# 24 of the 32 FFN down products in pairs by Strassen's seven products, with operands kept in DRAM, and merge planes loaded through staging

## The chip, the core and the metric

One core of one Trainium2 chip runs the whole program. TensorE multiplies, VectorE (DVE) and ScalarE (ACT) work element by element, GpSimd (POOL) and SyncE (SP) here mostly start transfers, and 16 DMA engines move data between DRAM and the on-chip memory. Each engine takes its instructions in a fixed order and waits where an input is not there yet. The metric is device time in microseconds of one execution, the median of several.

## What is computed

One step of a one-layer hybrid decoder for 1024 prompt tokens and 8 sample tokens, in 32-bit floating point. The part that the change concerns comes at the end of the layer:

```python
u  = sigmoid(ga + bma) * (o_hg @ w_br_a) + sigmoid(gb + bmb) * (y @ w_br_b)   # merge
x  = x + g1 * (u @ w_out)
h2 = rmsnorm(x, norm_mlp) * (1 + sc2) + sh2
x  = x + g2 * (square(relu(h2 @ w_up)) @ w_down)       # 1024 -> 4096 -> 1024
y  = rmsnorm(x, norm_final)
```

## The kernel before

**Layout.** Activations are kept transposed: a plane is 128 features (partitions) by 1032 token columns (1024 of the prompt, 8 samples). 1024 features are 8 planes (KD = 8). A 32-bit value is split in two float32r parts, hi (a rounded copy by ACT) and lo (the rest, a subtraction by DVE); a product of two such operands is three matmuls: wh by lo, wl by hi, wh by hi.

**A dense product** (`dense`, `dense_split`, L78 to L97) makes one output plane of 128 features from 8 input planes. `load_w` (L46) brings a 128x1024 weight block through one of three staging buffers `wr` (`stage`, L42) and splits it into `wh` (ACT, L53) and `wl` (DVE, L55); each of these has two buffers. The columns are done in three slices of 344, so a product is 3 x 8 x 3 = 72 matmuls of 344 columns, all on L86. PSUM has three `acc` banks for it. `DenseK` (L99) does the same work input plane by input plane (matmuls on L114), so that it can begin while later planes are still being loaded; it occupies all three `acc` banks until it ends.

**A Strassen pair** (`strassen_pair`, L1076) makes two output planes at once by seven products of half-size blocks (Winograd's form with few sums) in the order 1, 7, 6, 2, 5, 4, 3. Each product is two column quarters (q = 0, 1) of 258, of 4 x 3 = 12 matmuls each: 168 matmuls of 258 columns for a pair, on L1103. `strassen_weights` (L1035) forms the sums of the weight blocks and their splits (DVE on L1049 and L1061, ACT on L1059 to L1071) in tiles that share the two `wh` and two `wl` buffers. Products 1, 6 and 7 are copied out of PSUM by ACT (`keep`, L1092) before their bank goes on accumulating; products 2, 5, 4 and 3 each complete a quarter of the output, which `evac` takes out.

**The order of the work** is laid down at build time by a planner that gives each engine its sequence: of the instructions whose inputs it takes to be ready, the one that stands first in the program, where code inside `high_priority(AHEAD)` counts as standing 2000 instructions earlier. Weight loads and splits, evacuations and the sums of `strassen_weights` all stand in such blocks, so among them the place in the program decides. Matmuls, the sums of squares and the final norm have their plain place. The engines then keep the planned order, whatever really comes late.

**The stages in order.** `phase_merge` (L872): the two branch products and the gates. Each input plane is loaded by `load_split` (L837), which sends the raw data straight to the place of the lo plane and splits it there (ACT L844, DVE L845). `phase_out` (L961): the `w_out` product, x1 (8 planes that stay on the chip) and h2. `phase_ffn` (L1118): 32 up products, the first six dense (during which the sums of h2 for Strassen are made), then 13 Strassen pairs; the squared relu of each quarter is made in `evac` (DVE L1158, L1159, L1133; ACT L1132) and stored in DRAM, `ad`, by SP (L1129). Then 32 down products, 8 for each of four chunks c of 1024 inner features, all dense; planes of `ad` are loaded back and split (`act`, L1166, by `load_split`), 8 for the first chunk just when the down stage begins. Each product is added to x1 under its gate (`gated_add`, L933, DVE L937). The last chunk goes by column slices: for each of three slices 8 products, whose squares are summed (`sum_sq`, L950, L951), then the final norm (`rstd_model`, L1195) and the store of the output.

**Planes on the chip.** `PlanePool` (L1203) has planes under the names A (16), D (4), E (6) and L (14); a new plane takes the place of an older one when all its readers are done.

Of the kernel before, what the change touches and what calls it, by code (L numbers as in the profile page):

```python
# [17 lines left out]
P = 128  # L18
T = 1024
NB = 8  # L20
# [25 lines left out]
def load_w(k, src, prio=AHEAD):  # L46

    nc = k.nc
    with k.tc.high_priority(prio):
        wr = stage(k)[:, :KD * P]  # L50
        nc.sync.dma_start(wr, src)
        wh = k.wp.tile([P, KD * P], F32R, tag="wh", name="wh", bufs=2)
        nc.scalar.activation(wh, wr, AF.Copy)  # L53
        wl = k.wp.tile([P, KD * P], F32R, tag="wl", name="wl", bufs=2)
        nc.vector.tensor_tensor(wl, wr, wh.bitcast(F32), op=ALU.subtract)  # L55
    return wh, wl
# [42 lines left out]
class DenseK:  # L99


    def __init__(self, k, srcs, evacs, n=KD, prio=AHEAD):
        self.k, self.evacs, self.n, self.i = k, evacs, n, 0
        self.ws = [load_w(k, src, prio) for src in srcs]
        self.accs = [[k.ps.tile([P, 512], F32, tag="acc", name="acc", bufs=3) for _ in range(NS)],
                     [rec_ps(k, "acc2") for _ in range(NS if len(srcs) > 1 else 0)]]
# [730 lines left out]
def load_split(k, src, tag):  # L837
# [95 lines left out]
def gated_add(k, s, dst, base, ps, gate):  # L933

    nc = k.nc
    n = SW if s < NS - 1 else SW - NB
    nc.vector.scalar_tensor_tensor(dst[:, :n], ps[:, :n], gate[:, 0:1], base[:, :n], ALU.mult, ALU.add)  # L937
    if n < SW:
        t = k.sp.tile([P, NB], F32, tag="ga", name="ga", bufs=2)
        nc.vector.tensor_tensor(t, ps[:, n:], gate[:, 1:9], op=ALU.mult)  # L940
        nc.vector.tensor_tensor(dst[:, n:], t, base[:, n:], op=ALU.add)

# [133 lines left out]
def strassen_pair(k, srcs, X, evac):  # L1076
# [18 lines left out]
    for p, b in ((1, 1), (7, 2), (6, 1), (2, 3), (5, 1), (4, 2), (3, 1)):  # L1095
        for q in range(2):
# [8 lines left out]
            with k.tc.high_priority(AHEAD):  # L1105
# [8 lines left out]
                else:  # L1114
                    evac(0, 1, q, None, acc)


def phase_ffn(k, x1, h2):  # L1118
    nc = k.nc
    NF = 4 * KD  # L1120
    up = k.i["w_up"]
    ad = [k.dp.tile([P, NT], F32, name="ad%d" % j) for j in range(NF)]
    bufs = iter(range(1 << 20))

    def out(j, cols):
        n = next(bufs) % 4
        pool, tag = (k.sp2, "mt") if n < 2 else (k.sp, "sq")
        r = pool.tile([P, SW], F32, tag=tag, name="r", bufs=2)[:, :cols.stop - cols.start]
        return r, lambda: nc.sync.dma_start(ad[j][:, cols], r)  # L1129

    def relu2(r, ps):
        nc.scalar.activation(r, ps, AF.Relu)  # L1132
        nc.vector.tensor_tensor(r, r, r, op=ALU.mult)  # L1133

    def evac_up(j):
        def f(s, ps):
            r, store = out(j, cs(s))
            relu2(r, ps)
            store()
# [11 lines left out]
    for n in range(6, NF, 2):  # L1151
        def evac(m, half, q, a, ps, n=n):
            c = half * HN + q * HQ
            r, store = out(n + m, slice(c, c + HQ))
            if a is None:
                relu2(r, ps)
            else:
                nc.vector.tensor_tensor(r, a, ps, op=ALU.add)  # L1158
                nc.vector.scalar_tensor_tensor(r, r, 0.0, r, ALU.max, ALU.mult)  # L1159
            store()  # L1160
        strassen_pair(k, (up[n], up[n + 1]), X, evac)
# [4 lines left out]
    def act(c, j):  # L1166
        tag = "A" if c % 2 == 0 else "Q2" if j < 4 else "Q3"
        return load_split(k, ad[c * KD + j], tag)
    down = k.i["w_down"]
    aX = []  # L1170
    d = DenseK(k, (down[0],), (add(0),))
    for j in range(KD):
        with k.tc.high_priority(AHEAD):
            aX.append(act(0, j))
        d.step(*aX[j])
    for c in range(4):
        nX = []
        for m in range(KD):
            if c == 3:
                break  # L1180
            if c or m:
                dense(k, down[c * KD + m], aX, add(m))
            nX.append(act(c + 1, m))
        if c < 3:
            aX = nX
    for s in LAST:
        acc = k.sp2.tile([P, SW], F32, tag="sqa", name="sqa", bufs=1)
        for m in range(KD):
            w = load_w(k, down[3 * KD + m])
# [182 lines left out]
```

## Time and profile before

| | us |
|---|---|
| median of 3 runs (2532.47 to 2538.55) | 2536.15 |
| the profiled execution | 2534.51 |
| its span, first to last instruction | 2532.7 |
| TensorE busy | 2477.3 (98%) |
| DVE busy | 1754.1 (69%) |
| ACT busy | 1064.2 (42%) |

The profile is of one execution. A busy time counts instructions from start to end; consecutive matmuls overlap, so how fast TensorE goes is read from how many matmuls begin in a stretch, not from their durations. In the same way DVE instructions that do not depend on each other begin some 0.08 us before the one ahead has ended. The stages stand in these places of the span: merge from 1437, w_out from 1723, up products from 1816, the 13 Strassen pairs from 1884.8 to 2146.4, down products from 2146.4 to 2519.5, and the end of the last norm and stores to 2532.7.

### The profile page before, as it was taken

Reading aid. Unit: us, or ns where it says so; the run is one execution under the profiler, and the core shown is the slowest. Engines: PE = TensorE matmul, PEld = TensorE weight load, DVE = VectorE, ACT = ScalarE, POOL = GpSimd, SP = SyncE. Lnnn points to the kernel's source line nnn. Section 1 sums busy time; section 2 is a strip of 40 time slices with the busy share of each in tenths; the row PEclk is TensorE's granted clock in tenths of the full one; section 3 lists DMA queues with packets and bytes.
Section 4 is the critical chain, followed back from the end, with each engine's and each line's share of the span. In section 5 each row is a group of like instructions: output and inputs, shape, how many; then the busy total and the mean of one; then the engine's idle time right before and its main releaser. Section 6 shows DMA issues by size and latency. Waiting matters only on the chain.

```text
span 2532.7 us, 47468 instructions
## 1 busy us (share of the span) xinstructions
PE 2477.3 (98%) x19782; PEld 2409.1 (95%) x19782; DVE 1754.1 (69%) x3513; ACT 1064.2 (42%) x1574; POOL 4.2 (0%) x16
## 2 busy tenths in 40 slices
PE   6999999999999999999999999999999999999998
PEld 5999999989999999999999899999999999999997
DVE  7788888886678687787787733356976666443356
ACT  4455555554453544544535522123533334221123
POOL 0000000000000000000000000000000000000000
PEclk9999999999999999999999999999999999999999
DMA  6322222223334243243344634223233335332234
GB/s 256 125 95 98 94 99 102 101 97 101 102 110 139 82 145 128 97 148 120 101 145 135 229 111 151 76 101 125 98 109 112 105 105 158 129 116 84 75 103 147
DMA packets 114678, 300.94 MB, mean 119 GB/s; under 512 B 19056, under 2 KB 41648, under 8 KB 114448
## 3 DMA queue, kind: packets, MB, share of 16 engines
q1 hardware_dynamic: 113920, 296.91, 34.9%
q8 instruction: 155, 2.54, 0.4%
q0 software_dynamic: 112, 0.66, 0.1%
q14 instruction: 59, 0.48, 0.1%
q10 hardware_dynamic: 432, 0.35, 0.0%
HBM read 241.02 MB, written 57.10 MB: 118 GB/s over the span
## 4 chain that ended last, share of the span: by engine, by line
PE 73%; DVE 2%; DMA 1%; ACT 1%; issue 0%; SPq 0%; DVEq 0%; ACTq 0%
PE acc L86 56%; PE b L1103 10%; PE y_ps L795 1%; PE acc L114 1%; PE yi_ps L799 1%; PE kvx_ps L759 1%; DMA lo<-od 1%; PE xt_ps L747 1%; PE cb_ps L729 1%; DVE wl L55 1%; DMA lo<-ad 1%; DMA gt<-gd 0%; PE btok_ps L722 0%; PE ss L160 0%; ACT wh L53 0%
## 5 line engine op out<-in xcount | busy, mean ns | idle before, releaser
L86 PE MATMUL acc<-hl,wh 128*128 128x344 f32 x2232 | 721.8, 324 | 0.0
L86 PE MATMUL acc<-hh,wl 128*128 128x344 f32 x2232 | 721.1, 323 | 0.2 <-DVE wl L55 0.2
L86 PE MATMUL acc<-hh,wh 128*128 128x344 f32 x2232 | 717.2, 321 | 0.0
L86 PEld LDWEIGHTS acc<-hh,wh 128*128 128x128 f32 x2232 | 420.2, 188 | 2.9 <-issue 1.6
L86 PEld LDWEIGHTS acc<-hh,wl 128*128 128x128 f32 x2232 | 419.3, 188 | 3.8 <-issue 1.4
L86 PEld LDWEIGHTS acc<-hl,wh 128*128 128x128 f32 x2232 | 419.3, 188 | 3.4
L86 PE MATMUL acc<-hi,wl 128*128 128x344 f32 x1224 | 392.8, 321 | 2.3 <-DVE wl L55 2.3
L86 PE MATMUL acc<-lo,wh 128*128 128x344 f32 x1224 | 391.5, 320 | 1.4 <-ACT wh L53 1.4
L86 PE MATMUL acc<-hi,wh 128*128 128x344 f32 x1224 | 391.5, 320 | 0.0
L53 ACT ACTIVATE wh<-wr 128x1024 fp32r<-128x1024 f32 x198 | 208.8, 1055 | 416.0 <-PE acc L86 358.5
L55 DVE TENSOR_TENSOR wl<-wr,wh 128x1024 fp32r<-128x1024 f32 x198 | 242.1, 1223 | 202.7 <-ACT wh L53 201.6
L86 PEld LDWEIGHTS acc<-hi,wl 128*128 128x128 f32 x1224 | 230.5, 188 | 3.1 <-DVE wl L55 2.9
L86 PEld LDWEIGHTS acc<-lo,wh 128*128 128x128 f32 x1224 | 230.5, 188 | 2.0 <-ACT wh L53 2.0
L86 PEld LDWEIGHTS acc<-hi,wh 128*128 128x128 f32 x1224 | 230.9, 189 | 0.2
L937 DVE SCALAR_TENSOR_TENSOR x<-acc,modT,x 128x344 f32<-128x344 f32 (+1 forms) x120 | 68.6, 572 | 186.4 <-PE acc L86 185.7
L679 DVE SCALAR_TENSOR_TENSOR cv<-raw,cst,cv 128x1024 f32<-128x1024 f32 x96 | 122.7, 1278 | 0.0
L1103 PE MATMUL b<-tl,wh 128*128 128x258 f32 x416 | 117.5, 283 | 0.0
L1103 PE MATMUL b<-th,wl 128*128 128x258 f32 x416 | 117.3, 282 | 0.0
L1103 PE MATMUL b<-th,wh 128*128 128x258 f32 x416 | 117.3, 282 | 0.0
L671 ACT ACTIVATE raw<-acc 128x344 f32<-128x344 f32 x96 | 43.0, 457 | 125.2 <-PE acc L86 124.6
L844 ACT ACTIVATE hi<-lo 128x1032 fp32r<-128x1032 f32 x56 | 59.2, 1064 | 73.3 <-DMA lo<-ad 37.8
L1103 PE MATMUL b<-h2l,wh 128*128 128x258 f32 x312 | 88.4, 283 | 0.0
(280 smaller groups left out, 4339.6 us busy)
## 6 DMA issues: line engine op xcount, KB each, us to landing
wr<-w_ssm SPq DMA_DIRECT2D x48, 512.0 KB
wr<-w_down SPq DMA_DIRECT2D x48, 512.0 KB
wr<-w_ada SPq DMA_DIRECT2D x36, 512.0 KB
lo<-ad SPq DMA_DIRECT2D x32, 516.0 KB
wr<-w_hg SPq DMA_DIRECT2D x32, 512.0 KB
w<-cumd SPq DMA_DIRECT2D x32, 512.0 KB
wr<-w_up SPq DMA_DIRECT2D x32, 512.0 KB
ad<-r SPq DMA_DIRECT2D x104, 129.0 KB
```

The lines of the kernel that those rows point to most:

```text
L53: nc.scalar.activation(wh, wr, AF.Copy)
L55: nc.vector.tensor_tensor(wl, wr, wh.bitcast(F32), op=ALU.subtract)
L86: last = nc.tensor.matmul(acc[:M, :SW], a[:, sl], b[:, cs(s)], start=(i == 0 and j == 0), stop=(i == n - 1 and j == 2))
L114: k.nc.tensor.matmul(ac[s][:, :SW], a[:, sl], b[:, cs(s)], start=(i == 0 and j == 0), stop=(i == self.n - 1 and j == 2))
L671: dense(k, w, k.hX, lambda s, ps: nc.scalar.activation(raw[:, 3 + s * SW:3 + (s + 1) * SW], ps, AF.Copy))
L679: nc.vector.scalar_tensor_tensor(cv[:, :T], raw[:, j:j + T], cw[:, j:j + 1], cv[:, :T], ALU.mult, ALU.add)
L729: nc.tensor.matmul(ps[:, c * P:(c + 1) * P], Bc[:, cc], Cc[:, cc], start=True, stop=True)
L747: nc.tensor.transpose(ps[:, c * P:(c + 1) * P], x[:, cc * P:(cc + 1) * P], k.ident)
L759: nc.tensor.matmul(ps[:, c * P:(c + 1) * P], btok[:, cc], xdec[:, cc], start=True, stop=True)
L844: nc.scalar.activation(hi, raw, AF.Copy)
L937: nc.vector.scalar_tensor_tensor(dst[:, :n], ps[:, :n], gate[:, 0:1], base[:, :n], ALU.mult, ALU.add)
L1103: nc.tensor.matmul(acc, a[:, sl], x[:, cols], start=(p in (1, 7, 2) and i == 0 and j == 0), stop=(i == KD // 2 - 1 and j == 2), skip_group ...
```

## The change

Up stage: the 12 pairs of chunks 1 to 3 now pair plane i with plane i + 4 of their chunk, and their evacuation (`evac_sums`) keeps the four output quarters, makes Strassen's sums of them (four DVE subtractions for each of q = 0 and 1) and stores the seven operands of the down stage in DRAM (`cd`), 14 stores to a pair of 129 KB, from the GpSimd queue instead of SP's. The pair of planes 6 and 7 is stored as it is. x1 is stored to DRAM (`xd`) at the beginning of the phase and loaded again when the down stage begins.

Down stage: the first half of chunk 0 (4 planes) dense, by half-size weight blocks; chunks 1 to 3 by four Strassen pairs each; the second half of chunk 0 last, by column slices with half-size blocks (a 128x512 block for each of 24 products of 12 matmuls). The operands of Strassen are loaded with `operand`: 4 planes for each of seven products, 28 to a chunk, each 258 KB, one ACT copy and one DVE subtraction of 516 columns. Those for chunk 1 are loaded as the last up pair ends and during the dense half; those for the next chunk during the last pair of the chunk before, as each product lets go of its planes. The loads stand in `high_priority(AHEAD)` and come in the program ahead of what follows them.

Merge: `load_split` brings the raw plane through a staging buffer `wr` and splits it from there into hi and lo; the old form stays in the file under another name and has no caller.

```diff
@@ load_w and DenseK take n blocks @@
-def load_w(k, src, prio=AHEAD):
+def load_w(k, src, prio=AHEAD, n=KD):
-        wr = stage(k)[:, :KD * P]
+        wr = stage(k)[:, :n * P]
...
@@ load_split @@
-def load_split(k, src, tag):
+def load_split(k, src, tag, r=None):
+    if r is None:
+        r = stage(k)
+    k.nc.sync.dma_start(r, src)
+    return split_plane(k, r, tag)
...
@@ strassen_pair @@
-def strassen_pair(k, srcs, X, evac):
+def strassen_pair(k, srcs, X, evac, after=lambda p: None):
...
+        after(p)
@@ phase_ffn @@
+    HD = KD // 2
+    up, down = k.i["w_up"], k.i["w_down"]
+    ad = [k.dp.tile([P, NT], F32, name="ad%d" % j) for j in range(KD)]
+    cd = {(c, p, i): k.dp.tile([P, HN], F32, name="cd%d_%d_%d" % (c, p, i))
+          for c in range(1, 4) for p in ORDER for i in range(HD)}
+    xd = [k.dp.tile([P, NT], F32, name="xd%d" % m) for m in range(KD)]
+    for m in range(KD):
+        nc.sync.dma_start(xd[m], x1[m])
...
+    def evac_raw(m, half, q, a, ps):
+        c = half * HN + q * HQ
+        r = small(HQ)
+        relu2(r, a, ps)
+        nc.gpsimd.dma_start(ad[6 + m][:, c:c + HQ], r)
+    strassen_pair(k, (up[6], up[7]), X, evac_raw)
+    def evac_sums(c, i):
+        parts = {}
+        def sub(out, x, y):
+            nc.vector.tensor_tensor(out, x, y, op=ALU.subtract)
+        def f(m, half, q, a, ps):
+            if q not in parts:
+                t = [k.pp.tile([P, NT], F32, tag="L", name="ac").rearrange("p (n t) -> p n t", n=4)
+                     for _ in range(2)]
+                parts[q] = [x[:, n, :] for x in t for n in range(4)]
+            b11, b12, b21, b22, t1, t2, t4 = parts[q][:7]
+            r = parts[q][2 * m + half]
+            relu2(r, a, ps)
+            def store(p, x):
+                nc.gpsimd.dma_start(cd[c, p, i][:, q * HQ:(q + 1) * HQ], x)
+            if (m, half) != (0, 1):
+                store(1 + m + m * half, r)
+                return
+            sub(t1, b12, b11)
+            sub(b12, b22, b12)
+            sub(t2, b22, t1)
+            sub(t4, b21, t2)
+            for p, x in ((7, b12), (6, t2), (5, t1), (4, t4)):
+                store(p, x)
+        return f
+    tags = iter((("A",) * 16 + ("D",) * 4 + ("E",) * 6 + ("L",) * 6) * 4)
+    def plane(name):
+        return k.pp.tile([P, NT], F32R, tag=next(tags), name=name)
+    def operand(c, p):
+        r = []
+        with k.tc.high_priority(AHEAD):
+            for i in range(HD):
+                t = plane("x%d" % p)
+                hi, lo = t[:, :HN], t[:, HN:]
+                raw = lo.bitcast(F32)
+                nc.sync.dma_start(raw, cd[c, p, i])
+                nc.scalar.activation(hi, raw, AF.Copy)
+                nc.vector.tensor_tensor(lo, raw, hi.bitcast(F32), op=ALU.subtract)
+                r.append((hi, lo))
+        return r
+    def act(j):
+        with k.tc.high_priority(AHEAD):
+            hi, lo = plane("ah"), plane("al")
+            raw = lo.bitcast(F32)
+            nc.sync.dma_start(raw, ad[j])
+            nc.scalar.activation(hi, raw, AF.Copy)
+            nc.vector.tensor_tensor(lo, raw, hi.bitcast(F32), op=ALU.subtract)
+        return hi, lo
+    aX, Y = [], {}
+    def after_up(p):
+        if p == ORDER[0]:
+            aX.extend(act(j) for j in range(HD))
+        elif p == 5:
+            for n in ORDER[:2]:
+                Y[n] = operand(1, n)
+    for c in range(1, 4):
+        for i in range(HD):
+            j = c * KD + i
+            strassen_pair(k, (up[j], up[j + HD]), X, evac_sums(c, i),
+                          after_up if (c, i) == (3, HD - 1) else lambda p: None)
+    for n in ORDER[2:6]:
+        Y[n] = operand(1, n)
+    x1 = []
+    for m in range(KD):
+        x1.append(k.pp.tile([P, NT], F32, tag="L", name="x1"))
+        nc.sync.dma_start(x1[m], xd[m])
...
+    def evac_pair(j):
+        def f(m, half, q, a, ps):
+            n = 2 * j + m
+            c = half * HN + q * HQ
+            x = x1[n][:, c:c + HQ]
+            if a is not None:
+                r = small(HQ)
+                nc.vector.tensor_tensor(r, a, ps, op=ALU.add)
+                ps = r
+            gated_cols(k, x, x, ps, k.modT[:, 40 + n, :], HQ - NB if half and q else HQ)
+        return f
+    d = DenseK(k, (down[0][:, :HD * P],), (add(0),), HD)
+    for x in aX:
+        d.step(*x)
+    for m in range(1, KD):
+        w = load_w(k, down[m][:, :HD * P], n=HD)
+        for s in range(NS):
+            dense_split(k, w, aX, s, add(m))
+    Y[ORDER[6]] = operand(1, ORDER[6])
+    for c in range(1, 4):
+        Z = {}
+        def after(p, c=c, Z=Z):
+            n = ORDER.index(p)
+            if c < 3 and n < 6:
+                Z[ORDER[n + 1]] = operand(c + 1, ORDER[n + 1])
+            elif c == 3 and n == 0:
+                aX.extend(act(j) for j in range(6, KD))
+        for j in range(HD):
+            w = [down[c * KD + 2 * j + a] for a in range(2)]
+            if j < HD - 1:
+                strassen_pair(k, w, Y, evac_pair(j))
+                continue
+            if c < 3:
+                Z[ORDER[0]] = operand(c + 1, ORDER[0])
+            else:
+                aX.extend(act(j) for j in range(HD, 6))
+            strassen_pair(k, w, Y, evac_pair(j), after)
+        Y = Z
     for s in LAST:
...
-            w = load_w(k, down[3 * KD + m])
+            w = load_w(k, down[m][:, HD * P:], n=HD)
```

## Rows read from the trace of the kernel before

**Rows 1.** The profile's page: busy time of the engines; shares of the chain that ended last.
```profile
PE 2477.3 (98%) x19782; PEld 2409.1 (95%) x19782; DVE 1754.1 (69%) x3513; ACT 1064.2 (42%) x1574; POOL 4.2 (0%) x16
...
PE 73%; DVE 2%; DMA 1%; ACT 1%; issue 0%; SPq 0%; DVEq 0%; ACTq 0%
```

**Rows 2.** Stretches: busy time and instructions of each engine, granted clock, DMA share, GB/s.
```profile
1434.00:1470.00 36.00, 27.98 (x165) 25.56 (x164) 23.77 (x28) 26.68 (x30) 0.00 (x0) 1.00 0.88 339
1884.80:2146.40 261.60, 261.60 (x2185) 261.60 (x2184) 164.01 (x296) 93.01 (x171) 0.00 (x0) 1.00 0.37 113
2146.40:2176.00 29.60, 23.98 (x133) 22.73 (x132) 22.08 (x26) 15.01 (x16) 0.00 (x0) 0.88 0.76 280
2156.00:2166.00 10.00, 6.34 (x25) 5.62 (x26) 5.86 (x7) 5.32 (x5) 0.00 (x0) 0.73 1.01 403
2176.00:2460.00 284.00, 284.00 (x1807) 284.00 (x1806) 109.05 (x190) 52.22 (x55) 0.00 (x0) 1.00 0.26 86
2460.00:2519.60 59.60, 59.60 (x375) 58.75 (x374) 41.92 (x66) 23.42 (x35) 0.00 (x0) 1.00 0.48 154
```

**Rows 3.** Timeline of DVE where the second up pair meets the third: start, duration.
```profile
1922.39 0.42 DVE L1158 TENSOR_TENSOR r<-s,b 128x258 f32<-128x258 f32 x1 [0.54 <-PE b L1103]
1922.85 0.43 DVE L1159 SCALAR_TENSOR_TENSOR r<-r 128x258 f32<-128x258 f32 x1
...
1924.53 0.42 DVE L1133 TENSOR_TENSOR r<-r 128x258 f32<-128x258 f32 x1
1924.87 0.68 DVE L1061 TENSOR_TENSOR wr<-wr 128x512 f32<-128x512 f32 x1
1925.47 0.68 DVE L1049 TENSOR_TENSOR wl<-wr,wh 128x512 fp32r<-128x512 f32 x1
...
1928.28 1.22 DVE L1049 TENSOR_TENSOR wl<-wr,wh 128x1024 fp32r<-128x1024 f32 x1 [1.19 <-ACT wh L1064]
```

**Rows 4.** Timeline of ACT and DVE in the last up pair.
```profile
2138.69 1.05 ACT L844 ACTIVATE hi<-lo 128x1032 fp32r<-128x1032 f32 x1
...
2140.41 0.42 DVE L1158 TENSOR_TENSOR r<-s,b 128x258 f32<-128x258 f32 x1
2140.74 1.22 DVE L845 TENSOR_TENSOR lo<-lo,hi 128x1032 fp32r<-128x1032 f32 x1
2141.89 0.42 DVE L1159 SCALAR_TENSOR_TENSOR r<-r 128x258 f32<-128x258 f32 x1
```

**Rows 5.** Who waited for whom, 2146 to 2170: total, times, longest.
```profile
ACT hi L844 <- DMA lo<-ad: 8.5, 8, 2.5
...
PE acc L114 <- DVE lo L845: 4.1, 3, 1.9
```

**Rows 6.** Timeline of PE as the down stage begins.
```profile
2160.00 0.43 PE L114 MATMUL acc<-lo,wh 128*128 128x344 f32 x1 [1.91 <-DVE lo L845]
...
2161.46 0.49 PE L114 MATMUL acc<-lo,wh 128*128 128x344 f32 x1
2161.75 0.49 PE L114 MATMUL acc<-hi,wl 128*128 128x344 f32 x1
```

**Rows 7.** Timeline of ACT as the merge begins.
```profile
1450.25 1.07 ACT L844 ACTIVATE hi<-lo 128x1032 fp32r<-128x1032 f32 x1 [2.80 <-DMA lo<-od]
1451.52 1.06 ACT L868 ACTIVATE gt<-gt 128x1032 f32<-128x1032 f32 x1 [0.21 <-DMA gt<-gd]
1452.80 1.07 ACT L844 ACTIVATE hi<-lo 128x1032 fp32r<-128x1032 f32 x1 [0.22 <-DMA lo<-yd]
1454.09 1.07 ACT L844 ACTIVATE hi<-lo 128x1032 fp32r<-128x1032 f32 x1 [0.22 <-DMA lo<-od]
```

**Rows 8.** Timeline of PE as the first merge product ends.
```profile
1467.94 0.74 PE L86 MATMUL acc<-lo,wh 128*128 128x344 f32 x3 [0.67 <-ACT wh L53]
1470.15 0.42 PE L86 MATMUL acc<-hi,wl 128*128 128x344 f32 x1 [1.47 <-DVE wl L55]
```

**Rows 9.** Groups of DVE instructions, 2460 to 2532.7: busy, mean ns, idle before.
```profile
L937 DVE SCALAR_TENSOR_TENSOR x<-acc,modT,x 128x344 f32<-128x344 f32 x16 | 9.2, 573 | 12.4 <-PE acc L86 12.4
L951 DVE TENSOR_TENSOR sqa<-sqa,sq 128x344 f32<-128x344 f32 x15 | 7.6, 509 | 1.2 <-ACT sq L950 1.2
```

**Rows 10.** Timeline of DVE at the end: the last slice's final norm.
```profile
2525.75 3.99 DVE L1195 SCALAR_TENSOR_TENSOR x<-x,cst,nrm_y 128x344 f32<-128x344 f32 x8
```

**Rows 11.** Timeline of POOL: the later of its two transfers.
```profile
590.97 0.61 POOL L595 DMA_DIRECT2D late<-scv x1 [581.65 <-ACT o L494]
```

More of the change, by code (lines that the diff above doesn't have):

```diff
@@ L103, in __init__ @@
         self.k, self.evacs, self.n, self.i = k, evacs, n, 0
-        self.ws = [load_w(k, src, prio) for src in srcs]
+        self.ws = [load_w(k, src, prio, n) for src in srcs]
         self.accs = [[k.ps.tile([P, 512], F32, tag="acc", name="acc", bufs=3) for _ in range(NS)],
@@ L941, in gated_add @@
         nc.vector.tensor_tensor(dst[:, n:], t, base[:, n:], op=ALU.add)
+def gated_add(k, s, dst, base, ps, gate):
+    gated_cols(k, dst, base, ps, gate, SW if s < NS - 1 else SW - NB)
 def sum_sq(k, acc, x, first):
@@ L1115, in strassen_pair, with small, relu2 @@
                     evac(0, 1, q, None, acc)
+        after(p)
+ORDER = (1, 7, 6, 2, 5, 4, 3)
 def phase_ffn(k, x1, h2):
     nc = k.nc
-    NF = 4 * KD
-    up = k.i["w_up"]
-    ad = [k.dp.tile([P, NT], F32, name="ad%d" % j) for j in range(NF)]
-    bufs = iter(range(1 << 20))
[L1125 to L1133, printed above, removed]
+    HD = KD // 2
[6 more added lines that the diff above has]
+        nc.sync.dma_start(xd[m], x1[m])
+    bufs = iter(range(1 << 20))
+    def small(n):
+        pool, tag = (k.sp2, "mt") if next(bufs) % 4 < 2 else (k.sp, "sq")
+        return pool.tile([P, SW], F32, tag=tag, name="r", bufs=2)[:, :n]
+    def relu2(r, a, ps):
+        if a is None:
+            nc.scalar.activation(r, ps, AF.Relu)
+            nc.vector.tensor_tensor(r, r, r, op=ALU.mult)
+        else:
+            nc.vector.tensor_tensor(r, a, ps, op=ALU.add)
+            nc.vector.scalar_tensor_tensor(r, r, 0.0, r, ALU.max, ALU.mult)
     def evac_up(j):
         def f(s, ps):
-            r, store = out(j, cs(s))
-            relu2(r, ps)
-            store()
+            r = small(SW)
+            relu2(r, None, ps)
+            nc.gpsimd.dma_start(ad[j][:, cs(s)], r)
         return f
@@ L1150, in phase_ffn @@
     X = strassen_operands(h2, T)
[L1151 to L1161, printed above, removed]
+    def evac_raw(m, half, q, a, ps):
[3 more added lines that the diff above has]
+        nc.gpsimd.dma_start(ad[6 + m][:, c:c + HQ], r)
@@ L1169, in phase_ffn @@
-    down = k.i["w_down"]
-    aX = []
[L1171 to L1185, printed above, removed]
+    def evac_pair(j):
[5 more added lines that the diff above has]
+                r = small(HQ)
+                nc.vector.tensor_tensor(r, a, ps, op=ALU.add)
+                ps = r
+            gated_cols(k, x, x, ps, k.modT[:, 40 + n, :], HQ - NB if half and q else HQ)
+        return f
```

14 lines of the change are left out of this document (6 added, 8 removed).

## The prediction

> **What bounds the kernel now.** The page comes first: TensorE is busy 98% of the span and holds 73% of the chain that ended last, DVE 2% of it [rows 1]. A busy TensorE may still be a slow one, so the second view is that of stretches, read by how many matmuls begin in each [rows 2]. In the steady down stage 1807 begin in 284.00 us, 157.2 ns each for 344 columns; in the 13 up pairs 2185 in 261.60 us, 119.7 ns each for 258. TensorE is never idle in either and its granted clock is 1.00, so there the time is a count times a pitch, with DVE (38% and 63%), ACT and DMA beside it. Two stretches are not so. From 1434 to 1470, as the merge begins, 165 matmuls need 25.9 us and take 36.0: 10.1 lost, DMA share 0.88. From 2146.4 to 2176, as the down stage begins, 133 need 20.9 and take 29.6: 8.7 lost, and ten of these microseconds go at a DMA share of 1.01, 403 GB/s and a mean clock of 0.73. The waits name the path there: TensorE on the lo planes, ACT on the loads of `ad` [rows 5]. So three things need a price: the matmuls saved, the two poor starts, and what DVE is given, since it has a third of its time left in the pairs.
>
> **The products.** A dense pair is 144 x 157.2 ns = 22.63 us, a Strassen pair 261.60 / 13 = 20.12. Twelve pairs: 12 x 2.51 = **30.1 us less**. The eight products done in halves keep their 576 matmuls. This term is on the path everywhere and has no bounds worth naming.
>
> **The start of the down stage.** The four planes needed first are now asked for after product 1 of the last up pair, 17 us before TensorE wants them, and the stores no longer stand between these loads on SP. All of the 8.7 us can go, half-clock matmuls [rows 6] among them: **-8.7**, before what takes its place (below).
>
> **The merge start.** The planes of `od` reach ACT 3.84 us apart (1450.25, 1454.09), with a gate and a `yd` plane between them, 1.28 us each [rows 7]: three transfers share what DMA gives, while a step of TensorE there is 18 x 0.157 = 2.83 us. Through staging, `yd` can't run ahead into free planes: it needs one of three buffers, for which `od` and the weights rank first. Of the 10.1 us, 0.67 + 1.47 = 2.1 are the wait for the next weights after the product that holds both weight buffers [rows 8]; that stays. So up to 8.0 go. Against it: a staged plane that waits for its place holds a buffer that a weight load wants; one more wait like [rows 8] would cost 2.1. Between -8 and +2 I take **-5**, nearer the gain, as the loads that crowd out `od` are plain in the rows.
>
> **Sums in the up pairs.** Each pair gives DVE eight subtractions of 258 columns as its product 3 ends. One costs 0.34 (1924.53 to 1924.87) where the next does not depend on it, 0.46 (1922.39 to 1922.85) where it does [rows 3]: 2.7 to 3.7 us. DVE has 20.12 - 164.01/13 = 7.5 us idle in a pair, but not there. The third pair begins at 1884.8 + 2 x 20.12 = 1925.04, its third product (6) 48 matmuls later, at 1930.8; the lo weights for it end at 1928.28 + 1.22 = 1929.5, some 1.4 us early with the next matmul that uses them [rows 3]. The sums stand earlier in the program than these weights and rank ahead. If all go first TensorE waits 2.7 to 3.7 less 1.4, up to 2.3 us in each pair; if none, 0. That rank decides, and how far, the last up pair shows: L845, ready at 2138.69 + 1.05 = 2139.74 and later in the program, let L1158 go ahead at 2140.41, and was then put between it and L1159, which needs L1158 [rows 4]. Sums that follow from each other leave such places, so some weight work slips between. I take 1.2 us a pair, 12 x 1.2 = **+14.4**, bounds 0 and 28.
>
> **Operands as the down stage begins.** 24 operand planes are loaded around the end of the last up pair. A split costs DVE 0.60 (1924.87 to 1925.47, 512 columns) [rows 3], 24 x 0.60 = 14.4 us, with the last sums and squares (10 x 0.34) 17.8. They stand ahead of the evacuation of the first dense product, which ends after 36 x 0.157 = 5.7 us and holds all three `acc` banks, and ahead of the second product's weights. If all go first, TensorE waits 17.8 - 5.7 = 12 us; they are wanted only after the dense half, 8 x 5.7 = 45 us on, so with another order it is 0. x1 comes by the same road: if its first plane lands behind the 24 (6.3 MB, 16 us at 403 GB/s [rows 2]) the wait is 10 us. I take **+9**, near the upper end, by the rank in [rows 4].
>
> **Operands between chunks.** In the last pair of chunks 1 and 2, 24 more splits, 14.4 us, are freed one product after the other and rank ahead of all evacuations and weights behind them. A down pair has about the DVE work of an up pair. Twenty splits (12.0 us) fall between the end of product 1 and the end of the pair, 17.2 us in which DVE has 17.2 x 0.37 = 6.4 idle; so it is 5.6 us late when the next pair wants weights, and the last four add 2.4. From 0 (put off; the planes are wanted a whole pair later) to 10 (late loads hold ACT and DVE in their order, as the 8.5 us of [rows 5] do now). I take 7.5, twice: **+15**.
>
> **The last slices.** A product is 12 matmuls, 1.89 us, where it was 3.77. DVE still splits a weight block (0.60), adds under the gate (573 ns, some 0.49 back to back) and adds the squares (509 ns, 0.43) [rows 9]: 1.52 us, and for each slice the final norm, 3.99 [rows 10], and about 1.5 of the sum's root. Per slice 8 x 1.52 + 5.5 = 17.7 us of DVE against 15.1 of TensorE, where it was 30.2. Two norms lie beside matmuls: 2 x 2.6 = 5.2, and the small sample operations some 2: **+7**, bounds 3 and 10.
>
> **At nothing:** the stores on POOL, 14 x 0.61 = 8.5 us of a pair's 20.1 on a queue with 4.2 us of work now [rows 1, 11]; SP, which loses them, has its weight loads freed of waits for DVE; the copy of x1 to DRAM, covered by a DMA share of 0.37 [rows 2]; ACT, 93.01/13 = 7.2 us of a pair's 20.1 [rows 2]. Without the cover of POOL's idle time it is the third rival.
>
> **The sum** is made on the profiled execution, 2534.5, of which 2532.7 is the span: -30.1 - 8.7 - 5 + 14.4 + 9 + 15 + 7 = +1.6, so 2536.1. The median of the runs is 1.6 above that execution: **2538 us**, practically no change. With every bound at its good end it is -30.1 - 8.7 - 8 + 3 = -43.8, at its bad end -30.1 - 8.7 + 2 + 28 + 12 + 20 + 10 = +33, more if the clock falls.
>
> **Rival 1, the added DVE work finds its idle time.** Over a whole pair there is room: 12.6 + 3 us of 20.1. If the planner puts sums and splits behind the next weights, 2 us are left of each of the three DVE terms and 4 of the last slices, 10 in all, against gains of 30.1 + 8.7 + 5 = 43.8: 2534.5 - 43.8 + 10 + 1.6 = **2502**. For it: no matmul waited in 13 pairs at 63% DVE. Against it: the rank in [rows 4].
>
> **Rival 2, DVE's order starves the weights.** The place is each seam: product 3 to product 1 of the next pair, and the start of each chunk. It decides as soon as more than the 1.4 us spare is put ahead of the weights. Then sums cost 28, the start 12, the seams 20, the end 9, and TensorE, after standing still for microseconds, goes on at half clock, 0.29 us a matmul (2161.46 to 2161.75) in place of 0.157 [rows 6]; the 22 such matmuls of the start now cost 2.9, three such places 9. Losses of 28 + 12 + 20 + 9 + 9 = 78 against the same gains: 2534.5 - 43.8 + 78 + 1.6 = **2570**. For it: the work is fixed and greedy order is what the rows show; against it: all four at their bad end at once.
>
> **Rival 3, POOL can't keep up beside DVE.** If POOL could start transfers only while DVE stands still, 20.1 - 12.6 - 2.7 = 4.8 us of a pair, its 8.5 are 3.7 short; the sums' planes stay full and evacuation waits: 12 x 3.7 = 45 in place of 14, **2569**. No row shows it: POOL's second transfer took 0.61 us to issue [rows 11], and no other stands beside a busy DVE. The Trainium skill, SBUF — State Buffer, section SBUF: two separate sides, warns of just this: transfers issued from GpSimd starve while DVE holds the port pair they share. Its section Who interferes with whom narrows it to copies and the like in a two-port mode and takes tensor_tensor out, so by the page, too, this is unlikely; no run here shows it so far.
>
> **How the numbers follow.** Chances: the forecast 0.40 (2522 to 2554), rival 1 0.36, rival 2 0.20, rival 3 0.04. The line between change and none is 0.2%, about 5 us, what a measurement of this kernel can tell: 2531.1 and 2541.2. Faster: 0.34 of rival 1's 0.36 and a fifth of the forecast's 0.40, 0.42; same: two fifths of the forecast, 0.16, and the rest of rival 1, 0.18; slower: two fifths of the forecast and rivals 2 and 3, 0.40. The range leaves out the lower quarter of rival 1 and half of rivals 2 and 3: 2496 to 2570.
>
> **What would show it.** The down pairs at 20.1 us each and the dense halves at 157 ns a matmul: the first term. Waits of TensorE on L1049 or L1061 at the beginning of up pairs, near 1.2 us: the sums. A standstill of some 9 us some 6 us into the down stage, TensorE on the gated add: the operands. Longer pairs at the turn of each chunk. Matmuls of `od` 2.83 us a step: staging. The prediction is wrong if up pairs stay at 20.1 (then rival 1) or if the pairs inside a chunk are longer than 20.1, for which I name no reason.

## The result, and the profile after

| | before | changed |
|---|---|---|
| median, us | 2535.63 (5 runs, 2532.47 to 2538.55) | 2547.22 (5 runs, 2545.05 to 2549.68) |
| profiled execution / its span, us | 2534.51 / 2532.7 | 2545.05 / 2543.3 |
| TensorE, DVE, ACT, POOL busy, us | 2477.3, 1754.1, 1064.2, 4.2 | 2454.4, 1898.0, 1131.8, 108.2 |

The ratio is 1.0049, 95% interval 1.0036 to 1.0062: slower by half a per cent, 10.5 us between the two profiled executions. TensorE is busy for 23 us less and the program takes longer all the same. The page of the changed kernel, beside [rows 1]: DVE is now 6% of the chain that ended last, where it was 2%.

```profile
PE 2454.4 (97%) x20070; PEld 2383.2 (94%) x20070; DVE 1898.0 (75%) x3897; ACT 1131.8 (45%) x1753; POOL 108.2 (4%) x210
...
PE 68%; DVE 6%; issue 2%; ACT 1%; DMA 1%; POOL 0%; DVEq 0%; POOLq 0%; ACTq 0%
```

Where the time went is read from stretches, as in [rows 2] (columns: length, then busy time and instructions of TensorE, its weight loads, DVE, ACT, POOL; granted clock, DMA share, GB/s):

```profile
1434.00:1470.00 36.00, 34.80 (x219) 34.09 (x218) 22.48 (x31) 24.66 (x27) 0.00 (x0) 1.00 0.86 285
1895.66:1915.83 20.17, 20.17 (x170) 20.17 (x169) 12.61 (x24) 6.91 (x14) 4.32 (x8) 1.00 0.32 106
1915.83:2149.36 233.53, 227.32 (x1851) 223.14 (x1849) 171.60 (x344) 79.77 (x148) 82.46 (x154) 1.00 0.44 146
2149.36:2154.86 5.50, 5.50 (x38) 5.50 (x36) 4.28 (x9) 4.69 (x10) 0.00 (x0) 1.00 1.04 398
2154.86:2172.28 17.42, 0.30 (x2) 0.04 (x2) 15.50 (x30) 10.04 (x18) 4.27 (x8) 0.63 1.00 340
2172.28:2213.79 41.51, 41.51 (x252) 41.51 (x253) 19.94 (x46) 4.44 (x7) 0.00 (x0) 0.95 0.43 146
2213.79:2274.26 60.47, 60.47 (x506) 60.47 (x505) 43.86 (x87) 22.02 (x41) 0.00 (x0) 1.00 0.26 87
2274.26:2326.24 51.98, 43.87 (x338) 43.24 (x337) 42.81 (x83) 27.72 (x51) 0.00 (x0) 0.93 0.53 184
2366.58:2416.74 50.16, 42.20 (x338) 41.79 (x337) 42.77 (x81) 27.39 (x49) 0.00 (x0) 0.93 0.55 190
2523.90:2543.30 19.40, 1.88 (x5) 0.58 (x3) 12.89 (x27) 3.00 (x6) 0.00 (x0) 0.61 0.41 145
```

The merge now begins 219 matmuls where 165 began. One up pair with nothing ahead of it takes 20.17 us; the eleven that follow a pair with sums take 233.53 / 11 = 21.23. The first dense product of the down stage runs without a gap, then TensorE stands still for 17.1 us (17.42 between two starts) while DVE works for 15.5 of them. Three down pairs inside a chunk take 60.47 / 3 = 20.16; the two pairs around a turn of chunks take 51.98 and 50.16 where two undisturbed ones take 40.3. Behind the last matmul of a product there are 19.4 us.

Who held it, in the waits from 2149.4 to 2172.4 (sum, times, longest), and four lines of DVE's timeline from there (start, duration):

```profile
PE acc L86 <- DVE x L943: 17.1, 1, 17.1
```

```profile
2153.43 2.51 DVE L1232 TENSOR_TENSOR x<-x 128x516 fp32r<-128x516 f32 x4
2155.86 1.44 DVE L1192 TENSOR_TENSOR ac<-ac 128x258 f32<-128x258 f32 x4
...
2160.98 4.33 DVE L1232 TENSOR_TENSOR x<-x 128x516 fp32r<-128x516 f32 x7
...
2171.56 1.53 DVE L943 SCALAR_TENSOR_TENSOR x<-acc,modT,x 128x344 f32<-128x344 f32 x3
```

The gated add that frees the three banks (L943) comes after the operand splits (L1232) and the last sums (L1192); in [rows 5] TensorE waited there 4.1 us for planes of its own product.

**A measure for all runs.** The loss of a stretch is its length less its matmuls at the undisturbed pitch (157.2 ns for 344 columns, 119.75 for 258), counted from the starts in each run's trace. "Seam" is the last up pair and the dense half (for the kernel before: the start of its down stage); "end" is what follows the last pair (before: all that follows the start of its down stage), less its matmuls. The merge begins at any time between 1435.0 and 1440.8 in the profiled executions of these runs, so runs are compared by their medians and stages by their losses; where the turns of chunks were left as they are, the loss of the down pairs still varies between 22.1 and 24.5.

| run | median | merge | 12 up pairs | seam | 12 down pairs | end |
|---|---|---|---|---|---|---|
| before | 2535.6 | 14.7 | 0.2 | 8.7 | | 15.3 |
| changed | 2547.2 | 4.6 | 11.3 | 20.3 | 22.1 | 20.8 |
| staging in the merge alone, on before | 2524.1 | 4.6 | 0.6 | | | |
| the same, yd only | 2530.6 | 10.4 | 1.0 | | | |
| sums left out | 2533.1 | 4.7 | 0.6 | 16.9 | 22.5 | 21.8 |
| sums ranked later | 2536.1 | 4.6 | 0.6 | 18.7 | 23.1 | 21.8 |
| 16 planes spread over the dense half | 2546.9 | 4.6 | 11.3 | 17.6 | 23.9 | 21.3 |
| their splits ranked later | 2547.0 | 4.6 | 11.2 | 21.1 | 23.3 | 21.3 |
| x1 first | 2553.7 | 4.6 | 11.3 | 24.4 | 24.1 | 21.0 |
| x1 first and planes spread | 2540.3 | 4.6 | 11.2 | 12.9 | 22.3 | 21.9 |
| splits at the turns ranked later | 2538.2 | 4.6 | 11.2 | 18.4 | 14.4 | 20.8 |
| last weights split once | 2543.3 | 4.6 | 11.2 | 20.3 | 24.5 | 15.5 |
| all orders together | 2506.0 | 4.6 | 0.6 | 14.9 | 5.8 | 15.9 |
| the same, x1 in two halves | 2499.1 | 4.6 | 0.6 | 5.2 | 4.5 | 15.3 |

From before to changed: products -30.2, merge -9.4 (where the up pairs begin), up pairs and seam +11.1 and +11.6, down pairs +22.1, end +5.5: +10.7, the difference of the spans but for rounding. (The merge loses 10.1 less, but its first product begins 0.8 later, at 1437.50. Of the 15.3 at the end before, 0.7 are lost ahead of the last slices; from the first matmul of the last slices on it is 14.6, so these alone cost 6.1 more.)

### The profile page after: what moved, and what is told of

It reads as the page before. It is cut to its first block, busy times and chain, and to the rows that moved or that the text cites. A ratio compares the mean times of both kernels' runs of the same rounds, so it can differ in the third digit from the quotient of the medians.

```text
span 2543.3 us, 49043 instructions
## 1 busy us (share of the span) xinstructions
PE 2454.4 (97%) x20070; PEld 2383.2 (94%) x20070; DVE 1898.0 (75%) x3897; ACT 1131.8 (45%) x1753; POOL 108.2 (4%) x210
## 4 chain that ended last, share of the span: by engine, by line
PE 68%; DVE 6%; issue 2%; ACT 1%; DMA 1%; POOL 0%; DVEq 0%; POOLq 0%; ACTq 0%
PE acc L86 44%; PE b L1114 16%; PE acc L114 2%; PE y_ps L795 1%; PE yi_ps L799 1%; PE kvx_ps L759 1%; DVE ac L1192 1%; DVE x L1232 1%; DVE wl L1060 1%; PE xt_ps L747 1%; DVE wl L55 1%; PE cb_ps L729 1%; POOL cd L1204 0%; DMA x<-cd 0%; DVE x L1317 0%
## 5 line engine op out<-in xcount | busy, mean ns | idle before, releaser
L55 DVE TENSOR_TENSOR wl<-wr,wh 128x1024 fp32r<-128x1024 f32 (+1 forms) x182 | 205.6, 1130 | 192.5 <-ACT wh L53 190.5
L53 ACT ACTIVATE wh<-wr 128x1024 fp32r<-128x1024 f32 (+1 forms) x182 | 178.1, 979 | 201.9 <-PE acc L86 156.3
L1114 PE MATMUL b<-x,wh 128*128 128x258 f32 x1344 | 246.7, 286 | 4.3 <-ACT wh L1070 3.3
L1114 PEld LDWEIGHTS b<-x,wh 128*128 128x128 f32 x1344 | 211.3, 192 | 4.9 <-ACT wh L1070 3.7
L1114 PE MATMUL b<-x,wl 128*128 128x258 f32 x672 | 192.3, 286 | 11.8 <-DVE wl L1060 11.8
L86 PE MATMUL acc<-hi,wl 128*128 128x344 f32 x480 | 153.6, 320 | 1.3 <-DVE wl L55 1.3
L86 PE MATMUL acc<-lo,wh 128*128 128x344 f32 x480 | 153.2, 321 | 1.4 <-ACT wh L53 1.4
L86 PE MATMUL acc<-hi,wh 128*128 128x344 f32 x480 | 153.3, 319 | 0.0
L1060 DVE TENSOR_TENSOR wl<-wr,wh 128x512 fp32r<-128x512 f32 (+1 forms) x125 | 112.7, 901 | 46.4 <-ACT wh L1075 26.1
L1114 PEld LDWEIGHTS b<-x,wl 128*128 128x128 f32 x672 | 129.3, 192 | 12.2 <-DVE wl L1060 12.2
```

Of the source, the lines that this page charges most:

```text
L86: last = nc.tensor.matmul(acc[:M, :SW], a[:, sl], b[:, cs(s)], start=(i == 0 and j == 0), stop=(i == n - 1 and j == 2))
L1060: nc.vector.tensor_tensor(out, x, y, op=ALU.subtract)
L1114: nc.tensor.matmul(acc, a[:, sl], x[:, cols], start=(p in (1, 7, 2) and i == 0 and j == 0), stop=(i == KD // 2 - 1 and j == 2), skip_group ...
```

## The experiments

**Staging in the merge**, on the kernel before (the planes of `ad` keep the old way; `od` and `yd` hold the inputs of the two branch products, `o_hg` and `y`, in DRAM):

```diff
+def load_split(k, src, tag):
+    r = stage(k)
+    k.nc.sync.dma_start(r, src)
+    return split_plane(k, r, tag)
```

> The kernel before with one part of the change: planes of the merge come through staging. Theory: staging alone is what shortens the merge. In the profiled execution of the changed kernel TensorE loses 4.6 us between the start of the merge and the end of the w_out product, where the kernel before loses 14.9; so about 10 us less here too: 2526 us, up pairs at 20.13 and the start of the down stage as before (about 9 us lost). Rival: the gain comes from elsewhere in the changed program (another order of the whole); then 2532 to 2536 and a loss in the merge of 10 us or more.

Measured: 2524.1 us, ratio 0.9965 (0.9949 to 0.9980); merge loss 4.6, up pairs at 20.17. Staging alone is the whole gain of the merge.

**Only yd through staging**, `od` as before:

```diff
-            oX.append(load_split(k, k.od[i], "A"))
+            oX.append(load_split_in(k, k.od[i], "A"))
```

> As the run beside it, but the planes of od keep the old way (straight to the place of the lo plane); only yd comes through staging. Theory A: the gain is bandwidth, since a staged yd can no longer run ahead of od; then nearly all of the 10 us stay: 2526 to 2528. Theory B: od itself profits, since its load begins before its place is free; then little is left: 2533 to 2536, a loss in the merge near 14.

Measured: 2530.6 us, ratio 0.9981 (0.9972 to 0.9990). It lies between the theories: of the 10.1 us of merge loss 4.3 go. TensorE still waits three times for planes of `od`:

```profile
PE acc L114 <- DVE lo L852: 3.4, 3, 1.7
ACT hi L851 <- DMA lo<-od: 3.7, 5, 2.5
```

(sum, times, longest, 1437 to 1464). The last of the eight planes of `od` is asked for at 1451.56 in the kernel before, at 1449.00 here, and at 1445.17 in the changed kernel, where there is no such wait. So it is both: with `yd` held back 4.3 of the 10.1 us go, and the other 5.8 go only when `od`, too, need not wait for its place. No run stages `od` alone.

**Without the sums**, on the changed kernel:

```diff
-            sub(t1, b12, b11)
-            sub(b12, b22, b12)
-            sub(t2, b22, t1)
-            sub(t4, b21, t2)
-            for p, x in ((7, b12), (6, t2), (5, t1), (4, t4)):
+            for p, x in ((7, b12), (6, b22), (5, b11), (4, b21)):
```

> The changed kernel without Strassen's sums of the up outputs: the four DVE subtractions for each of q = 0 and 1 are left out, and the quarters themselves are stored as the operands 7, 6, 5 and 4 (14 POOL stores to a pair as before). The output is another. Theory: DVE's sums ahead of the next weights cost the up pairs 1.1 us each; without them 20.13 a pair, 11 x 1.1 = 12 us less, and the wait as the down stage begins is shorter by up to 8 x 0.36 = 2.9: 2532 us. Rival: the stores on POOL or their DMA traffic cost it; then pairs stay at 21.2 and the time at 2544 to 2547.

Measured: 2533.1 us. The pairs of chunks 1 to 3 take 20.16 us each, beside the same stores on POOL (eleven pairs):

```profile
1898.80:2120.60 221.80, 221.80 (x1850) 221.80 (x1849) 138.56 (x254) 75.91 (x144) 82.49 (x154) 1.00 0.43 143
```

So the 1.1 us are the subtractions, not the stores or their traffic. At the seam 16.9 us stay without any sum, most of them now as one wait of 10.0 us of the first dense product for its lo weights (DVE L55).

**The same sums, later in the order:**

```diff
+            with k.tc.high_priority(-400):
                 sub(t1, b12, b11)
                 ... (the other sums and the stores)
```

> The changed kernel with the same sums and stores, but ranked 400 instructions later by the planner, behind the weights of the next pair. Theory: it is the order and not the amount that costs; up pairs 20.13 to 20.3, 10 to 12 us less: 2535 to 2537, with the wait as the down stage begins as long as now or up to 3 us longer. Rival: DVE has too much work in a pair, whatever its order; then pairs stay over 20.9 and the time over 2543.

Measured: 2536.1 us, up pairs 20.17 with all sums in them. Not the amount, the place. DVE as the fourth up pair begins, first in the changed kernel (start, duration; x6 is six sums), then with the sums later:

```profile
1938.13 2.11 DVE L1192 TENSOR_TENSOR ac<-ac 128x258 f32<-128x258 f32 x6
1940.16 0.68 DVE L1060 TENSOR_TENSOR wl<-wr,wh 128x512 fp32r<-128x512 f32 x1
1940.76 0.42 DVE L1192 TENSOR_TENSOR ac<-ac 128x258 f32<-128x258 f32 x1
1941.10 0.69 DVE L1060 TENSOR_TENSOR wr<-wr 128x512 f32<-128x512 f32 x1
```

```profile
1939.75 0.69 DVE L1060 TENSOR_TENSOR wl<-wr,wh 128x512 fp32r<-128x512 f32 x1
1940.35 0.42 DVE L1158 TENSOR_TENSOR ac<-ac 128x258 f32<-128x258 f32 x1
1940.69 0.69 DVE L1060 TENSOR_TENSOR wr<-wr 128x512 f32<-128x512 f32 x1
1941.29 1.44 DVE L1192 TENSOR_TENSOR ac<-ac 128x258 f32<-128x258 f32 x4
```

In the first, six sums pass ahead of the lo weights of product 7, the second of the pair (L1060 at 1940.16), and TensorE, at 1940.90, has waited 0.56 us for them; in the second the sums go behind them. Counted from start to start some 0.8 of the 1.1 us are lost there, the rest at product 6.

**The seam, 1: planes spread.**

```diff
-    for n in ORDER[2:6]:
-        Y[n] = operand(1, n)
...
             dense_split(k, w, aX, s, add(m))
+        if 2 <= m < 6:
+            Y[ORDER[m]] = operand(1, ORDER[m])
```

> The changed kernel, with the operands of products 6, 2, 5 and 4 for chunk 1 (16 of the 24 planes at the start of the down stage) asked for one product at a time during the dense half, after its products 2 to 5. Both their loads and their splits move. Theory: the 19.2 us that TensorE loses at the start fall to 2 to 5 us: 2530 to 2533. Rival: x1 or the last sums hold the first gated add for their own reasons; then 8 us or more stay: 2537 or more.

**The seam, 2: their splits later.**

```diff
+                with k.tc.high_priority(-back):          # back = 300 for these 16 planes
                     nc.scalar.activation(hi, raw, AF.Copy)
                     nc.vector.tensor_tensor(lo, raw, hi.bitcast(F32), op=ALU.subtract)
```

> The changed kernel; the loads of the same 16 planes are asked for as early as now, but their splits (ACT copy and DVE subtraction) are ranked 300 instructions later. Theory A: DVE's order alone makes the standstill; then it goes from 17.3 to 4 us or less: 2530 to 2534. Theory B: the transfers make it, 24 planes of 258 KB with the next weights and x1 behind them in SP's queue; then 8 to 12 us of it stay: 2538 to 2542.

Measured: 2546.9 and 2547.0 us, no less than the change. The standstill was 14.5 and 18.5 us where it had been 17.3: in the first the rival held, something else keeps the gated add; in the second theory A fell, and theory B had the right kind and too small a size. The first edit moved less than it was meant to. Ten of the 16 planes were still asked for before x1, so that x1 stood behind 18 loads in place of 24 (SP's timeline, start and duration; three more operand loads stand between the second line and the third):

```profile
2144.32 4.28 SPq L1230 DMA_DIRECT2D x<-cd  x8
...
2149.22 5.63 SPq L1230 DMA_DIRECT2D x<-cd  x7
...
2161.86 6.15 SPq L1260 DMA_DIRECT2D x<-xd  x8
```

What ended the standstill with the splits later (DVE, start and duration):

```profile
2157.20 6.15 DVE L1233 TENSOR_TENSOR x<-x 128x516 fp32r<-128x516 f32 x10
2165.91 3.72 DVE L1233 TENSOR_TENSOR x<-x 128x516 fp32r<-128x516 f32 x6 [2.57 <-ACT x L1232]
2170.31 1.53 DVE L943 SCALAR_TENSOR_TENSOR x<-acc,modT,x 128x344 f32<-128x344 f32 x3 [0.68 <-DMA x<-xd]
```

The gated add (L943) waits for x1. Its loads stand outside `high_priority`, so SP issues them behind every operand load, here from 2163.97. The splits, ranked later, still came first, and the first plane of x1 had landed only 0.68 us after they ended. In the changed kernel this plane is asked for at 2160.96, and the trace shows no wait for it; there, as in the first of these two runs, the add stands behind splits in DVE's order.

**The seam, 3: x1 first,** the 24 planes as in the change:

```diff
     def after_up(p):
         if p == ORDER[0]:
             aX.extend(act(j) for j in range(HD))
+            with k.tc.high_priority(AHEAD):
+                for m in range(KD):
+                    x1.append(k.pp.tile([P, NT], F32, tag="L", name="x1"))
+                    nc.sync.dma_start(x1[m], xd[m])
...
-    x1 = []
-    for m in range(KD):
-        x1.append(k.pp.tile([P, NT], F32, tag="L", name="x1"))
-        nc.sync.dma_start(x1[m], xd[m])
```

> The changed kernel with one thing else: the loads of x1 stand ahead of the operand loads, inside the block that ranks them 2000 instructions earlier; in the changed kernel they stand outside it, and came last in SP's queue, also where the operands' loads (16 planes) or their splits had been moved back, which took nothing off the standstill of TensorE beyond 3 us. Theory: this rank of x1 holds the first gated add, and it is planned behind all splits for that reason; with x1 there, the standstill of 17.3 us falls to 4 to 9 us (sums and the splits that have arrived still go first): 2533 to 2541. Rival: the splits stand ahead by their own rank, and all 24 of them; then 12 us or more stay: 2542 or more.

Measured: 2553.7 us, slower than the change. The standstill stays at 16.9 us, the rival's case, with another name on it (waits, 2147 to 2178; SP's timeline):

```profile
PE acc L86 <- ACT wh L53: 16.8, 1, 16.8
```

```profile
2146.39 25.00 SPq L1230 DMA_DIRECT2D x<-cd  x24
2171.49 21.16 SPq L51 DMA_DIRECT2D wr<-w_down  x7
```

x1 is there, but the first gated add still begins only at 2172.47, behind the splits, and the next weights are asked for at 2171.49, behind 24 loads. Besides, x1's 4.2 MB now crowd the planes of the dense half: between the last up pair and the end of the first dense product some 4 us more are lost.

**The seam, 4: both,** the two diffs above (planes spread, x1 first):

> The changed kernel with two of its orders moved, and nothing else: x1 is loaded first, and 16 of the 24 operand planes are asked for one product at a time in the dense half. Each of the two alone left the standstill after the first dense product at 14.5 and 16.9 us. Theory: there are two locks, x1 at the end of SP's queue and the splits ahead of the gated add on DVE, and either of them alone is enough to hold TensorE; with both gone the standstill is 2 to 4 us, with up to 5 us more lost ahead of it, where the loads of x1 crowd those of the dense half: 2533 to 2539. Rival: a third cause (the last sums, or DVE being full) holds it; then 8 us or more of standstill stay: 2541 or more.

Measured: 2540.3 us, ratio to before 1.0020 (1.0011 to 1.0030). The standstill is 3.7 us (waits, 2149 to 2170: sum, times, longest):

```profile
PE acc L86 <- DVE x L943: 4.0, 2, 3.6
```

Ahead of it 2.6 us are lost and 1.5 at half clock, behind it 2.2 on the next weights and 2 at half clock. So the theory of two locks held, at a time 1 us above its range, and to undo either lock alone was worth nothing or less. What the second lock is made of stays open in part: spreading moves loads and splits together. With x1 first alone the splits held the gated add until 2172.47, and the next weights, behind the loads on SP, held TensorE until 2177.27.

**The turns:** splits of `operand(c + 1, ...)`, all but the first product's, ranked 200 later.

```diff
-                Z[ORDER[n + 1]] = operand(c + 1, ORDER[n + 1])
+                Z[ORDER[n + 1]] = operand(c + 1, ORDER[n + 1], 200)   # back, as above
```

> The changed kernel with the splits of the operands that are loaded at the turns of chunks 1 and 2 (six of seven products) ranked 200 instructions later, so behind the weights of the next pair. Theory: order, not amount: the turns, which cost 11.7 and 9.8 us now, cost 0 to 3 each: 2526 to 2531. Rival: the splits are needed as soon as they can be had, or DVE's work of the two pairs is too much; then 5 us or more stay at each turn: 2535 or more.

Measured: 2538.2 us; the turns cost 7.5 and 6.3 us where they cost 11.7 and 9.9. The time is the rival's; the order of the splits is about a third of the loss. What TensorE waits for at the first turn, 2284 to 2308 in the changed kernel, and 2293 to 2306 here:

```profile
PE b L1114 <- DVE wl L1060: 5.9, 1, 5.9
PE b L1114 <- ACT wh L1070: 1.3, 1, 1.3
```

```profile
PE b L1114 <- ACT wh L1070: 3.8, 1, 3.8
ACT wh L1070 <- DVE wr L1060: 1.5, 1, 1.5
```

The weights of the next pair are still late (SP's timeline):

```profile
2275.79 16.15 SPq L1230 DMA_DIRECT2D x<-cd  x24
2292.04 1.07 SPq L1064 DMA_DIRECT2D wr<-w_down  x2
```

SP asks for them behind 24 operand loads, two microseconds before the pair begins. DVE has filled the time with splits, five of them just ahead of the sum (L1060, at 2299.40) that ACT waits for.

**The last slices:** their eight weight blocks split once, into planes that are free by then.

```diff
...
-            w = load_w(k, down[m][:, HD * P:], n=HD)
-            dense_split(k, w, aX, s, add(m))
+            dense_split(k, W[m], aX, s, add(m))      # W: loaded and split in the last pair
```

> The changed kernel with the eight weight blocks of the last column slices loaded and split once, during the last Strassen pair, and kept in free planes, in place of three times. DVE loses 16 of 24 splits there, 16 x 0.60 = 9.6 us. Theory: DVE is what ends last in the last slices (its end lies 19.3 us behind the last product, 13.2 in the kernel before): about 6 us less: 2541. Rival: the tail is the norm and its stores alone; then 2546 to 2548.

Measured: 2543.3 us; the end falls from 20.8 to 15.5, behind the last matmul of a product 14.0 us stay:

```profile
2529.70:2543.70 14.00, 1.18 (x5) 0.34 (x3) 7.15 (x15) 2.02 (x4) 0.00 (x0) 0.68 0.29 101
```

DVE was what ended last, as the theory has it; the turns of this run, which the edit leaves alone, lost 2.4 us more.

**All orders together:** sums later, x1 first, planes spread, operands at the turns 200 later with their loads too, last weights once.

> The changed kernel with what the other runs point to, together: sums ranked 400 later; x1 loaded first; the 16 operand planes asked for one product at a time in the dense half; the operands at the turns of chunks, loads and splits, ranked 200 later (with the splits alone ranked later, the next pair's weights still stood behind 24 loads in SP's queue, and 8 and 6 us were lost at the turns); the weights of the last slices split once. Theory: order alone makes the losses, so up pairs 20.13 (12 us less), 2 to 5 us of standstill at the start of the down stage in place of 19, 0 to 4 at each turn in place of 11.7 and 9.8, and 5 less at the end: 2495 to 2505. Rival: DVE or the transfers have too little room however they are ordered: single stages keep over half of their losses, 2515 or more.

Measured: 2506.0 us, ratio 0.9894 (0.9878 to 0.9911), a microsecond above the range. The turns cost 5.8 in all, the up pairs nothing; the seam keeps 14.9, 4.8 of it waits for planes of the dense half behind x1.

**The same, x1 in two halves:** four planes in the last up pair, four in the dense half; the last pair's sums only 60 later.

```diff
+            load_x1(range(HD))                       # in after_up
...
+        if m < 3:                                    # in the dense half
+            load_x1(range(2 + 2 * m, 4 + 2 * m))
```

> As the run with everything together, but only four of the eight planes of x1 are loaded in the last up pair, the other four in the dense half, and the sums of the last pair are ranked only 60 later (they free the planes for these four). Theory: the 4.8 us that TensorE lost waiting for planes of the dense half as the down stage began came from x1's 4.2 MB in front of them; with half of it 1 to 3 us stay: 2501 to 2505. Rival: the planes come late for another reason, or the second four of x1 come too late for the fifth product: 2506 to 2512.

Measured: 2499.1 us, ratio 0.9856 (0.9833 to 0.9878): faster than both kernels, 36 us below the one before. The 13 up pairs, the dense half, the down pairs, the end:

```profile
1878.70:2141.00 262.30, 262.30 (x2187) 262.29 (x2185) 190.75 (x381) 91.47 (x170) 89.66 (x167) 1.00 0.45 149
2141.00:2192.00 51.00, 46.72 (x295) 45.72 (x294) 42.45 (x90) 21.26 (x37) 5.33 (x10) 1.00 0.72 261
2192.00:2440.00 248.00, 246.06 (x2030) 244.58 (x2029) 198.47 (x393) 111.57 (x202) 0.00 (x0) 1.00 0.37 126
2440.00:2497.90 57.90, 45.36 (x279) 43.56 (x277) 41.13 (x95) 16.32 (x34) 0.00 (x0) 0.92 0.21 74
```

DVE does the same sums and operand splits as in the change and is busy for 191 us in the up pairs and 198 in the down pairs, with 4.5 us of loss left in the latter; TensorE's clock does not fall in any of the first three stretches.

## Why the prediction was right or wrong

The forecast was 2538 with 2522 to 2554 as its own range; 2547.2 lies in it. The side was left open, 0.42 faster to 0.40 slower, and the forecast's middle was 9 us too low. In part that is luck: measured less forecast, the terms are off by +10.2 (start), +6.5 (turns), -4.4 (merge), -2.3 (sums) and -1.5 (last slices), which cancel in part, and the first three lie outside their own bounds.

- **The products** (-30.1): -30.2. Inside a chunk the down pairs run at 20.16, as the up pairs of [rows 2] did.
- **The old start** (-8.7): gone as forecast; the first dense product runs at full pitch. What the loads of `ad` gained is lost again when x1 is put ahead of them.
- **The merge** (-5, bounds -8 and +2): -9.4, outside. The step that failed: I counted a fixed 2.1 for the weights after the first product [rows 8], which became 1.2 (0.68 and 0.52), and looked only to 1470, where the kernel before still had twelve matmuls at half clock to come, 1.6 us that went as well. And the reason was half the truth: `yd` held back gives 4.3, the rest comes when `od` is staged too.
- **The sums** (+14.4): +12.1. The mechanism and the rank were as read from [rows 4], the size in part by luck: I took the spare time of product 6, and most of the loss came a product earlier, on the lo weights of product 7. Eleven pairs pay 1.1 us, not twelve: the last pair's sums fall into the seam.
- **The operands at the start** (+9, bounds 0 and 12): 17.3 of standstill and 1.9 at half clock, 19.2 in all, above the upper bound. This is the step that failed most. I priced two queues, DVE (12) and x1 behind the 24 planes (10), and took +9, less than either. Both queues were there, and with either undone alone TensorE still stood for 14.5 us or more. In the changed kernel, between 2149.36 and the first gated add at 2171.56 DVE did 23 splits (13.8), eight sums (2.9), two squares (0.7) and two weight splits (1.2), and stood 3.0 us waiting for planes. My 17.8 us of work was nearly right (18.6). But I let it begin with all planes there, while DMA moved 340 to 398 GB/s and ACT could begin on the last four only at 2167.26; and I took off 5.7 us of cover, in 1.2 of which DVE stood idle.
- **The operands between chunks** (+15, bounds 0 and 20): +21.5 at the two turns, just above the upper bound. The mechanism was right, but a term was missing: the next pair's weights wait in SP's queue behind the same 24 loads. I had counted the splits on DVE and late loads on ACT, and not the loads on SP. With the splits alone put later 13.8 of the 21.6 us stayed; with the loads put later too, the down pairs lost 5.8 in all. And after the first standstill 27 matmuls go at 0.215 us in place of 0.12, 2.8 us with the first of them.
- **The last slices** (+7): +5.5, or +6.1 counted from their first matmul in both kernels; DVE ends last, as said.
- **At nothing:** held for the stores on POOL, not for SP. POOL issues 14 stores a pair at 0.54 us each while DVE is busy 74% of the time, and pairs with later sums are at 20.17. So the third rival is out. The Trainium skill, SBUF — State Buffer, section Who interferes with whom, names tensor_tensor among what did not stall transfers, although with two inputs in SBUF it takes the read side of the shared ports; these rows agree. SP I put at nothing because it loses the stores; the operand loads filled its queue again, and the next weights stood behind them at the turns.
- **The rivals.** The first asked for sums and splits behind the next weights and gave 2502; where the order was made so, with x1 moved and the last weights split once, 2499 and 2506 were measured. It was the right price for a program that the planner doesn't make by itself. The second had the right places (seams, half clock), too high a price for the sums (28 for 12.1) and too low a one for the start (12 for 17.3); its matmuls at half clock in the old start number 17 in the trace, 2.3 us, and not 22.

What stays open: two of the late splits at the seam are put down by the trace to stores of `cd`, 1.2 to 1.7 us each; no run took these stores away. Nor did a run separate splits from loads in the second lock of the seam.

## What to carry to other kernels

Work that is given to an engine with idle time costs nothing only if it stands behind the work that TensorE waits for in that engine's fixed order: here much the same sums and splits cost 54 us or 10 (up pairs, seam and down pairs of the table) by the order of work and loads. A burst of loads is a queue on three engines at once (SP, ACT, DVE), so list what stands behind it on each, the next weights and the load left at plain rank above all. Where two such locks hold the same wait, undoing one can show nothing, so undo them together before a cause is thrown out.

## What the runs showed of the hardware

After a standstill TensorE went on at the lower of its two clock levels (1.2 in place of 2.4 GHz), 0.29 us for 344 columns and 0.215 for 258: 13 matmuls after 17.1 us of standstill, 27 and 12 after the 6.0 us at each turn. The first of these in the changed kernel (PE, start and duration):

```profile
2172.28 0.63 PE L86 MATMUL acc<-al,wh 128*128 128x344 f32 x1 [17.12 <-DVE x L943]
...
2173.28 0.49 PE L86 MATMUL acc<-al,wh 128*128 128x344 f32 x1
2173.57 0.49 PE L86 MATMUL acc<-ah,wl 128*128 128x344 f32 x1
```

In the last run, after 1.9 us, one matmul took 0.24 and the next ones went at 0.157. In the run with everything together, after waits of 1.8, 0.2 and 0.9 us close behind each other, 19 went at 0.287. In the changed kernel the half clock added 1.4 to 2.8 us to each of the three long waits, which I had priced only in a rival.
